# A conformer-and-attention step: the output weights of the convolution layer are split ahead of time, kept in DRAM, and used by column halves

## The chip, the cores and the metric

The kernel runs on one core of a Trainium2 chip. The metric is the device time of one execution in microseconds (us). TensorE (PE) does the matmuls, VectorE (DVE), ScalarE (ACT) and GpSimd (POOL) the elementwise work, and SyncE (SP) issues nearly all DMA transfers, in one queue of its own, in order.

## The reference, cut to what matters

Two layers over 256 context tokens (the prompt, "p") and 2048 latent tokens (the sample, "s"), width 1024. The first layer is a convolution branch, and only it and its output product matter here:

```python
def modulate(x, g, shift, scale):
    return rms_norm(x, g) * (1 + scale[:, None]) + shift[:, None]
...
    # layer 0, in words: h = modulate(x); three products of h with conv_w_in give u's two factors and z;
    # a depthwise convolution of 31 taps runs along the tokens; then
    #   y = silu(layer_norm(conv)) * silu(z);  x = x + gate * (y @ conv_w_out)
```

Everything is float32. A product of float32 matrices is made of three matmuls: each operand is split into a rounded high part and the rest, and high*high, high*low and low*high are summed.

## The kernel before

**The convolution layer** (`conv_layer`) takes the tokens in two chunks: chunk 0 holds the prompt and s0 to s1023, chunk 1 holds s1024 to s2047. Each chunk has 8 steps, one for each 128 channels (some 41 us a step in chunk 0). A step multiplies its blocks of tokens with three parts of the input weights, 24 matmuls for a block of 512 tokens (`ci_ps`, L356 to L358). DVE and ACT empty the product's PSUM banks (`u`, L456 on DVE; `z`, L459 on ACT; and others), and PE can write a bank again only when it has been emptied. The 31 taps of the step before run meanwhile: most on DVE (`cv`, L507, and the join L511), some as a scaling on ACT (`cv_p`, L485) with an addition on POOL (L488), summed and joined at the end (`cv_s`), and stored to `vc_d`. What each of PE, ACT, DVE and POOL does, and in which order, is fixed by a list of events with planned times (`at(time, piece)`); SP's queue follows from it. An engine that must wait holds back everything behind it on its list. A DVE operation that comes late so makes the ACT operation that needs it late, and with it all that stands behind that one on ACT. Weights come through two buffers of 512 KB ("raw"), and `ci_wh` (ACT, L426) and `ci_wl` (POOL) are the two halves that the matmuls read.

**The seam.** After the last step of chunk 1 the output product begins (`conv_out_pipeline`): tiles of 128 tokens, p0, p128, s0, s128 and so on, each as two column halves of 512 (a "job" below) in two quarters of 12 matmuls. A quarter takes 4 of the 8 row blocks of the weights: first `wh*yh` and `wl*yh` in turn (L826, L827), then four times `wh*yl` (L829). The layer norm of later tiles runs between the quarters; its first PE operation of a tile is the mean, `ln_s_mu` (L700), and later `ln_s_rb` (L720). The order on PE is that of the code. The output weights come through `out_weight`: eight raw loads of 512 KB, for each an ACT copy to the high part `co_h` (L752) and a DVE subtraction for the rest `co_l` (L112, helper `rest_dve`), into four buffers of 2 MB ("slot"): hi and lo of row blocks 0 to 3, and of 4 to 7. The program places this at the seam, where DVE and POOL also work on the last taps (steps 6 and 7 of chunk 1). The PSUM space of the layer norm is that of the convolution's accumulators, and comes free when the last join (`cv_7_0`, DVE L511) is done. The slots are the ones that the convolution layer used for its activations (`B[0]`, the block before the last), for the last `adaw` weights (of the modulation, used by `ada_ps`, L221), and for `ln_work`, the room in which POOL and DVE make the norm of s0.

Of the kernel before, what the change touches and what calls it, by code (L numbers as in the profile page):

```python
# [11 lines left out]
F32 = mybir.dt.float32  # L12
F32R = mybir.dt.float32r
# [5 lines left out]
P = 128  # L19
D = 1024  # L20
# [56 lines left out]
class Kern:  # L77
    def __init__(self, ctx, tc, io):
# [21 lines left out]
        self.gate_d = d("gate_d", [2, 2, D])  # L100
        self.rpb_d = d("rpb_d", [P + 1, RPB_PITCH])
        self.yp_d = d("yp_d", [NK, 2, P, NPR])


    def round_pool(self, out, src):
# [255 lines left out]
    def conv_layer(self, part_a, part_b):  # L361
# [267 lines left out]
        for j, (i, c) in enumerate([(0, 4), (0, 5)] + [(1, c) for c in range(6)]):  # L629
            g = self.ada_chunk(i, c)  # L630
            t = begin[NK + 1 + j] - ADA_TIME
            for dt in (-ADA_AHEAD, 0, 0.1, ADA_TIME - 0.5, ADA_TIME + ADA_LAG, ADA_TIME + ADA_LAG + 1.2)[: 6 if c < 4 else 5]:
                at(t + dt, step_of(g))

        for i, (load, rms, first, every, gap) in enumerate(((begin[3], begin[3] + 14, begin[3] + 26, 3.0, 30), (begin[7] + 3, begin[7] + 14, begin[8] - 7.6, 1.2, 9.6))):
            src, t0, n = part_b[i]
# [104 lines left out]
            pass  # L741
        return y[0]

    def out_weight(self, w, name, res):

        nc = self.nc
        for k in range(NK):
            if k % 4 == 0:
                hi, lo = (self.slot(F32R, f"{name}_{s}{k}", [P, NK // 2, D]) for s in "hl")
            raw = self.raw(w[k * P : k * P + P, :], [P, D], f"{name}_raw{k}")  # L750
            yield
            nc.scalar.copy(hi[:, k % 4, :], raw)  # L752
            self.rest_dve(lo[:, k % 4, :], raw, hi[:, k % 4, :])
            res[0].append(hi[:, k % 4, :])
            res[1].append(lo[:, k % 4, :])
            yield

    def conv_out(self, w, blocks, ready, res=None):

# [43 lines left out]
    def conv_out_pipeline(self, w, blocks, ready, ahead, res):  # L803
# [34 lines left out]
        def more():  # L838
            if prep:
                next(prep[0], None) or prep.pop(0)  # L840

        last = None
        for i in range(len(tiles) + 2):
            src, a = names[i]
            run = i < len(tiles)
            if run:
                x1[i] = self.t4(F32, f"x1_{src}{a}", [P, D]) if i < 2 else self.xp.tile([P, D], F32, tag="ln", name=f"x1_{src}{a}", bufs=5)
                nc.sync.dma_start(x1[i], self.tok_rows(src, a, P))
            t, before = i + 2, i + 1
            norm(t + 1, True)  # L850
            if run:
                pm = self.mm_bank(f"co_{src}{a}_0")
            if i == 0:
                quarter(i, 0, 0, pm)
                norm(t, True)
                norm(t)
            norm(t)
            norm(before)
            if 0 < i < len(tiles):
                quarter(i, 0, 0, pm)  # L860
            norm(t)
            norm(before)
            norm(t)
            norm(before)
            scale = None
            if last:
                residual(*last)
            norm(t)
            more()
            if run:  # L870
                quarter(i, 0, 1, pm)
            norm(t)
            norm(before)
            norm(t)
            if last:
                scale = self.store_x1(i - 1, names[i - 1], x1, tiles, prep, res)
                last = None
            norm(before)
            if run:
                residual(i, 0, pm)  # L880
                more()
                pm = self.mm_bank(f"co_{src}{a}_1")
                quarter(i, 1, 0, pm)
            norm(t)
            more()
            if run:
                quarter(i, 1, 1, pm)
                last = i, 1, pm
            norm(t)
            if scale:  # L890
                scale()
            norm(t + 1)
            more()
        for g in prep:
            for _ in g:
                pass
# [373 lines left out]
    def phase1(self):  # L1270
        tc = self.tc
        with ExitStack() as c:
# [5 lines left out]
            with tc.tile_pool(name="convp", bufs=2) as self.up, tc.tile_pool(name="acc", bufs=2, space=bass.MemoryType.PSUM) as self.pc:  # L1278
                E = mybir.EngineType
                ordered = {E.PE, E.Activation, E.DVE, E.Pool}  # L1280
                with tc.manual_schedule(engines=ordered):
                    self.conv_layer([("p", 0, 256), ("s", 0, 512), ("s", 512, 512)], [("s", 1024, 512), ("s", 1536, 512)])
                work = self.room[0]
                self.ready.append(self.conv_norm("s", 0, [work[:, i] for i in range(3)] + [self.t4(F32R, f"ln_s0_y{t}") for t in "hl"]))
                self.gate = [self.spread_row(self.t4(F32, f"gate0_{g}", [P, D]), self.gate_d[0, g]) for g in range(2)]
                w = [[], []]
# [77 lines left out]
    def bank(self, tag, name, bufs, n=512):  # L1364
        return self.ps.tile([P, n], F32, tag=tag, name=name, bufs=bufs)
# [394 lines left out]
```

## Time and profile before

| | |
|---|---|
| time, median of 3 runs | 2839.27 us (2832.55, 2839.27, 2840.76) |
| time of the profiled execution | 2836.73 us |
| its span from the first to the last instruction | 2834.9 us |
| PE busy | 2695.6 us, 95% of the span |
| DVE busy | 1849.0 us, 65% |
| ACT busy | 1450.4 us, 51% |
| POOL busy | 1502.8 us, 53% |
| mean granted clock of PE | 0.982 of full speed |

The shares are means over stages that differ much. The seam lies near 700 us; chunk 0 ends near 424 us. A busy PE at half clock does half the work.

### The profile page before, as it was taken

Reading aid. Unit: us, or ns where it says so; the run is one execution under the profiler, and the core shown is the slowest. Engines: PE = TensorE matmul, PEld = TensorE weight load, DVE = VectorE, ACT = ScalarE, POOL = GpSimd, SP = SyncE. Lnnn points to the kernel's source line nnn. Section 1 sums busy time; section 2 is a strip of 40 time slices with the busy share of each in tenths; the row PEclk is TensorE's granted clock in tenths of the full one; section 3 lists DMA queues with packets and bytes.
Section 4 is the critical chain, followed back from the end, with each engine's and each line's share of the span. In section 5 each row is a group of like instructions: output and inputs, shape, how many; then the busy total and the mean of one; then the engine's idle time right before and its main releaser. Section 6 shows DMA issues by size and latency. Waiting matters only on the chain. (4 is left out here: it accounts for less than half of the span.)

```text
span 2834.9 us, 45402 instructions
## 1 busy us (share of the span) xinstructions
PE 2695.6 (95%) x16079; PEld 2334.6 (82%) x16079; DVE 1849.0 (65%) x3126; ACT 1450.4 (51%) x2546; POOL 1502.8 (53%) x1631
## 2 busy tenths in 40 slices
PE   6999999999899999999999989879999999999998
PEld 4888877777677889899998878768888898888887
DVE  4789989999886510013457542157787787778885
ACT  4457565677554312134222244246676666667774
POOL 4679878888663343355113325235555555455564
PEclk9999999999899999999999999989999999999999
DMA  7233554555445554446789997788877787866753
GB/s 255 71 121 116 186 188 158 175 176 183 159 119 172 158 163 126 133 142 207 239 294 350 344 304 221 192 247 218 244 207 188 201 213 185 232 188 183 199 168 109
DMA packets 435627, 548.02 MB, mean 193 GB/s; under 512 B 42945, under 2 KB 306201, under 8 KB 435272
## 3 DMA queue, kind: packets, MB, share of 16 engines
q1 hardware_dynamic: 430080, 522.17, 61.5%
q10 hardware_dynamic: 5320, 22.95, 2.1%
q8 instruction: 128, 2.10, 0.3%
q14 instruction: 99, 0.81, 0.1%
HBM read 359.86 MB, written 189.22 MB: 194 GB/s over the span
## 5 line engine op out<-in xcount | busy, mean ns | idle before, releaser
L1514 POOL TENSOR_SCALAR sa_p<-sa_p,sa_m 128x992 f32<-128x992 f32 (+2 forms) x256 | 279.7, 1093 | 445.0 <-DVE sa_m L1513 319.0
L507 DVE SCALAR_TENSOR_TENSOR cv<-u,dw,cv 128x640 f32<-128x640 f32 (+2 forms) x570 | 427.8, 822 | 3.8 <-ACT cv L503 2.9
L1529 ACT CAST sa_pt<-sa_T 128x512 fp32r<-128x512 f32 (+3 forms) x512 | 275.2, 588 | 238.0 <-PE sa_T L1520 236.5
L112 DVE TENSOR_TENSOR sa_pt<-sa_T,sa_pt 128x512 fp32r<-128x512 f32 (+3 forms) x512 | 328.4, 682 | 3.5 <-ACT sa_pt L1529 3.0
L356 PE MATMUL ci_ps<-h_s_hi,ci_wh 128*128 128x512 f32 x768 | 307.1, 400 | 1.9 <-DVE shift L244 1.0
L358 PE MATMUL ci_ps<-h_s_hi,ci_wl 128*128 128x512 f32 x768 | 303.1, 395 | 0.0
L357 PE MATMUL ci_ps<-h_s_lo,ci_wh 128*128 128x512 f32 x768 | 302.9, 394 | 0.0
L1506 DVE TENSOR_REDUCE sa_m<-sa_S 128x1 f32<-128x512 f32 x256 | 176.1, 688 | 187.7 <-PE sa_S L1488 174.3
L1512 ACT ACTIVATE sa_p<-sa_S,sa_m 128x992 f32<-128x992 f32 (+2 forms) x256 | 267.3, 1044 | 50.7 <-DVE sa_m L1508 41.2
L1520 PE MATMUL sa_T<-ident,sa_p 128*128 128x128 f32 (+3 forms) x2048 | 272.4, 276 | 7.5 <-DVE sa_pt L112 6.8
L1520 PEld LDWEIGHTS sa_T<-ident,sa_p 128*128 128x128 f32 (+3 forms) x2048 | 239.7, 138 | 41.6 <-issue 11.3
L488 POOL TENSOR_TENSOR cv_s<-cv_s,cv_p 128x519 f32<-128x519 f32 (+1 forms) x155 | 233.2, 1504 | 69.7 <-DVE cv_s L511 48.9
L485 ACT ACTIVATE cv_p<-u,dw 128x640 f32<-128x640 f32 (+2 forms) x326 | 240.9, 770 | 54.7 <-POOL cv_s L488 35.8
L488 POOL TENSOR_TENSOR cv_p<-cv_p,cv_p 128x520 f32<-128x520 f32 (+1 forms) x155 | 227.8, 1470 | 26.7 <-ACT cv_p L485 19.1
L1549 PE MATMUL sa_O<-sa_pt,a_v 120*128 120x256 f32 (+5 forms) x1280 | 192.0, 280 | 0.0
L1544 PE MATMUL sa_O<-sa_pt,cv 128*128 128x256 f32 x1024 | 176.0, 294 | 4.2 <-DVE 1_0_of L1563 1.7
L356 PEld LDWEIGHTS ci_ps<-h_s_hi,ci_wh 128*128 128x128 f32 x768 | 145.5, 189 | 39.2 <-ACT cv_p L485 2.5
L1508 DVE CUSTOM_DVE_ANT_0 sa_S<-sa_S,a_bm,sa_m 128x480 f32<-128x480 f32 (+2 forms) x256 | 170.9, 668 | 9.1
L358 PEld LDWEIGHTS ci_ps<-h_s_hi,ci_wl 128*128 128x128 f32 x768 | 145.0, 189 | 33.6
L357 PEld LDWEIGHTS ci_ps<-h_s_lo,ci_wh 128*128 128x128 f32 x768 | 145.5, 190 | 31.1
L1549 PEld LDWEIGHTS sa_O<-sa_pt,a_v 120*128 120x128 f32 (+2 forms) x1280 | 168.8, 193 | 0.0
L356 PE MATMUL ni_s<-h_s_hi,nis_wh 128*128 128x512 f32 x384 | 152.1, 396 | 10.3 <-DVE ni_s_l L112 5.9
(843 smaller groups left out, 7181.6 us busy)
## 6 DMA issues: line engine op xcount, KB each, us to landing
adaw<-in_ada_w SPq DMA_DIRECT2D x24, 1024.0 KB
ci_w<-in_conv_w_in SPq DMA_DIRECT2D x48, 512.0 KB
a_bm<-bm_d SPq DMA_DIRECT2D x32, 720.0 KB
x_s<-in_x_sample SPq DMA_DIRECT2D x32, 512.0 KB
vs_d<-v_s SPq DMA_DIRECT2D x128, 128.0 KB
a_qh<-qh_d SPq DMA_DIRECT2D x128, 128.0 KB
a_ql<-ql_d SPq DMA_DIRECT2D x128, 128.0 KB
o_x<-x_d SPq DMA_DIRECT2D x32, 512.0 KB
```

Source lines behind the costliest of these rows:

```text
L112: self.nc.vector.tensor_tensor(out=lo, in0=src, in1=hi.bitcast(F32), op=ALU.subtract)
L356: self.nc.tensor.matmul(out, wh[:, k, :], hh[:, k, :], start=k == 0, stop=False)
L357: self.nc.tensor.matmul(out, wh[:, k, :], hl[:, k, :], start=False, stop=False)
L358: self.nc.tensor.matmul(out, wl[:, k, :], hh[:, k, :], start=False, stop=k == NK - 1)
L485: nc.scalar.activation(t, st["u"][:, c0 + tap : c1 + tap], AF.Copy, scale=self.dw[:, ct, tap : tap + 1])
L488: nc.gpsimd.tensor_tensor(out=st["sum", half], in0=st["sum", half], in1=st[half, tap], op=ALU.add)
L507: nc.vector.scalar_tensor_tensor(out=out, in0=u, scalar=w, in1=first, op0=ALU.mult, op1=ALU.add)
L1512: nc.scalar.activation(p[:, n], S[:, n], AF.Exp, scale=-1.0, bias=m[:, 2:3], accum_out=m[:, 3:4])
L1514: nc.gpsimd.tensor_scalar(out=p[:, n], in0=p[:, n], scalar1=m[:, 3:4], scalar2=1.0, op0=ALU.mult, op1=ALU.mult)
L1520: nc.tensor.transpose(t[:w, c * P : c * P + P], p[:, x + c * w : x + c * w + w], self.ident)
L1529: nc.scalar.copy(pt[:w, 0, part, :, at], t)
L1549: nc.tensor.matmul(dst, v[:w, c0 + c].rearrange("p s d -> p (s d)"), loc[:, lo:hi], start=False, stop=s == 1 and c == 3)
```

## The change

For each step k of chunk 0 a new generator, `split_out_weight(k)`, loads 128 rows of the output weights into a raw buffer, rounds them on ACT in two column halves, subtracts on DVE in place, and stores both parts to DRAM (`cw_d`, 8 MB in all, in 24 stores). `out_weight` then only loads: 16 transfers of 512 KB from `cw_d` into the four slots, a column half at a time. The first three tiles take turns: their jobs (tile, column half) run in the order (p0,0), (p128,0), (s0,0), (p0,1), (p128,1), (s0,1). The last sums of the modulation (`adat_ps`, `adao` and its store) move from the seam to the end of the pipeline's second round. The norm of s0 gets another buffer for its result.

```diff
+        for k in range(NK):
+            g = self.split_out_weight(k)
+            for dt in (15.0, 11.0, 10.0, 9.0):
+                at(begin[k + 1] - dt, step_of(g))
...
-    def out_weight(self, w, name, res):
-
-        nc = self.nc
-        for k in range(NK):
-            if k % 4 == 0:
-                hi, lo = (self.slot(F32R, f"{name}_{s}{k}", [P, NK // 2, D]) for s in "hl")
-            raw = self.raw(w[k * P : k * P + P, :], [P, D], f"{name}_raw{k}")
-            yield
-            nc.scalar.copy(hi[:, k % 4, :], raw)
-            self.rest_dve(lo[:, k % 4, :], raw, hi[:, k % 4, :])
...
+    def split_out_weight(self, k):
+
+        nc = self.nc
+        rows = slice(k * P, k * P + P)
+        raw = self.raw(self.io["conv_w_out"][0][rows, :], [P, D], f"co_raw{k}")
+        yield
+        his = []
+        for h in range(2):
+            cs = slice(h * 512, h * 512 + 512)
+            hi = self.st(F32R, f"co_h{k}_{h}", [P, 512])
+            nc.scalar.copy(hi, raw[:, cs])
+            nc.sync.dma_start(self.cw_d[0, rows, cs], hi.bitcast(F32))
+            his.append(hi)
+        yield
+        for h in range(2):
+            cs = slice(h * 512, h * 512 + 512)
+            self.rest_dve(raw[:, cs].bitcast(F32R), raw[:, cs], his[h])
+            if h == 0:
+                yield
+        nc.sync.dma_start(self.cw_d[1, rows, :], raw)
+
+    def out_weight(self):
+
+        tiles = [[self.slot(F32R, f"co_{s}{q}", [P, NK // 2, D]) for s in "hl"] for q in range(2)]
+        for h in range(2):
+            cs = slice(h * 512, h * 512 + 512)
+            for q in range(2):
+                for e in range(0, 4, 2):
+                    for s in range(2):
+                        r0 = (4 * q + e) * P
+                        src = self.cw_d[s, r0 : r0 + 2 * P, cs].rearrange("(k p) n -> p k n", p=P)
+                        self.nc.sync.dma_start(tiles[q][s][:, e : e + 2, cs].bitcast(F32), src)
+        return [[tiles[k // 4][s][:, k % 4, :] for k in range(NK)] for s in range(2)]
...
+        jobs = {0: [(0, 0), (1, 0)], 1: [(2, 0), (0, 1)], 2: [(1, 1), (2, 1)]}
...
+            if i == 1:
+                next(self.last_sums, None)
...
-                self.ready.append(self.conv_norm("s", 0, [work[:, i] for i in range(3)] + [self.t4(F32R, f"ln_s0_y{t}") for t in "hl"]))
+                y = self.slot(F32R, "ln_s0_y", [P, 2, NK, P], False)
+                self.ready.append(self.conv_norm("s", 0, [work[:, i] for i in range(3)] + [y[:, i] for i in range(2)]))
...
-                for _ in self.out_weight(self.io["conv_w_out"][0], "co", w):
-                    pass
+                w = self.out_weight()
```

**SP's queue at the seam.** The names: `vc_d` is the store of a finished convolution, `zc_d` that of `z`, `x_p` and `ln_s_v` are loads for the residual and for the norm. Before:

```order
L515 DMA vc_d<-cv_6_1_s 128x519
L461 DMA zc_d<-z_7_0_6323 128x512
L340 DMA co_raw_6523<-in_conv_w_out 128x1024
L340 DMA co_raw_6527<-in_conv_w_out 128x1024
L848 DMA x_p_6623<-in_x_prompt 128x1024
L686 DMA ln_s_v<-vc_d 128x8x128
L461 DMA zc_d<-z_7_1_6373 128x512
L232 DMA adao_5_6414<-in_ada_b 2x512
L340 DMA co_raw_6533<-in_conv_w_out 128x1024
```

And now (`co_h_6595` and `co_l_6596` are the two parts of row blocks 0 to 3, `co_h_6597` and `co_l_6598` those of 4 to 7):

```order
L516 DMA vc_d<-cv_6_1_s 128x519
L783 DMA co_h_6595<-cw_d 128x2x512
L783 DMA co_l_6596<-cw_d 128x2x512
L462 DMA zc_d<-z_7_0_6412 128x512
...
L783 DMA co_l_6596<-cw_d 128x2x512
L694 DMA ln_s_v<-vc_d 128x8x128
L462 DMA zc_d<-z_7_1_6462 128x512
L783 DMA co_h_6597<-cw_d 128x2x512 x4
L783 DMA co_l_6598<-cw_d 128x2x512 x4
L516 DMA vc_d<-cv_7_0_s 128x520
```

In the lines left out stand six more loads of row blocks 0 to 3. All eight of these (both column halves) go ahead of the first load of row blocks 4 to 7, and the four `co_l_6598` come last, ahead of the last two `vc_d`.

**POOL at the seam.** `ln_s_yh` and `ln_s_yl` are the two parts of the norm of s0, read from `ln_work`. Before, ahead of the additions of step 7:

```order
L106 TENSOR_SCALAR ln_s_yh<-ln_work 128x1024
L488 TENSOR_TENSOR cv_6_1_s<-cv_6_1_s,cv_6_1_p_6219 128x519
L109 TENSOR_TENSOR ln_s_yl<-ln_work,ln_s_yh 128x1024
L488 TENSOR_TENSOR cv_6_1_s<-cv_6_1_s,cv_6_1_p_6226 128x519
```

And now, as `ln_s_y`:

```order
L489 TENSOR_TENSOR cv_7_0_p_6396<-cv_7_0_p_6396,cv_7_0_p_6454 128x520
L107 TENSOR_SCALAR ln_s_y<-ln_work 128x1024
L489 TENSOR_TENSOR cv_7_0_p_6396<-cv_7_0_p_6396,cv_7_0_p_6459 128x520
L110 TENSOR_TENSOR ln_s_y<-ln_work,ln_s_y 128x1024
L489 TENSOR_TENSOR cv_7_0_p_6396<-cv_7_0_p_6396,cv_7_0_p_6467 128x520
```

The pair has moved behind six and seven of the eleven additions `cv_7_0_p`. The buffer `ln_work` becomes the slot of `co_l_6598`, so these four loads can only be issued behind the second of the pair.

**DVE in chunk 0**, near the end of step 4, with `cv_3_0_s` the join of the step before. Before:

```order
L112 TENSOR_TENSOR h_s_lo<-m_s_1_h_2365,h_s_hi 128x256
L507 SCALAR_TENSOR_TENSOR cv_3_0_0_2246<-u_3_1634,dw,cv_3_0_0_2246 128x640
L507 SCALAR_TENSOR_TENSOR cv_3_0_s<-u_3_1634,dw,cv_3_0_1_2251 128x640
L507 SCALAR_TENSOR_TENSOR cv_3_0_0_2246<-u_3_1634,dw,cv_3_0_0_2246 128x640
L112 TENSOR_TENSOR h_s_lo<-m_s_1_h_2405,h_s_hi 128x256
L511 SCALAR_TENSOR_TENSOR cv_3_0_s<-cv_3_0_0_2246,more,cv_3_0_s 128x640
```

And now:

```order
L113 TENSOR_TENSOR h_s_lo<-m_s_1_h_2412,h_s_hi 128x256
L113 TENSOR_TENSOR co_raw_2401<-co_raw_2401,co_h_0_2448 128x512
L508 SCALAR_TENSOR_TENSOR cv_3_0_0_2291<-u_3_1668,dw,cv_3_0_0_2291 128x640
L113 TENSOR_TENSOR co_raw_2401<-co_raw_2401,co_h_1_2451 128x512
L508 SCALAR_TENSOR_TENSOR cv_3_0_s<-u_3_1668,dw,cv_3_0_1_2296 128x640
L508 SCALAR_TENSOR_TENSOR cv_3_0_0_2291<-u_3_1668,dw,cv_3_0_0_2291 128x640
L113 TENSOR_TENSOR h_s_lo<-m_s_1_h_2458,h_s_hi 128x256
L512 SCALAR_TENSOR_TENSOR cv_3_0_s<-cv_3_0_0_2291,more,cv_3_0_s 128x640
```

Two subtractions of 128x512 now stand ahead of the join, as in each of the eight steps of chunk 0.

## Rows read from the trace of the kernel before

**Rows 1.** Page, the head: the span of the profiled execution.

```profile
span 2834.9 us, 45402 instructions
```

**Rows 2.** Windows at the seam: length, then busy PE, PEld, DVE, ACT, POOL; PEclk; DMA; GB/s.

```profile
710.00:720.00 10.00, 7.83 (x17) 4.15 (x17) 10.00 (x14) 6.75 (x10) 7.68 (x5) 0.68 0.64 210
720.00:730.00 10.00, 4.11 (x7) 2.21 (x8) 9.13 (x11) 5.69 (x9) 9.61 (x6) 0.67 0.43 136
```

**Rows 3.** Timeline of PE at the seam: start, duration, instruction [idle before, releaser].

```profile
701.90 0.39 PE L357 MATMUL ci_ps<-h_s_lo,ci_wh 128*128 128x512 f32 x1
702.14 0.40 PE L358 MATMUL ci_ps<-h_s_hi,ci_wl 128*128 128x512 f32 x1
702.46 1.93 PE L221 MATMUL ada_ps<-adaw,cs 128*32 128x512 f32 x16
710.87 1.87 PE L230 MATMUL adat_ps<-adam,sel 128*2 128x512 f32 x2 [6.49 <-ACT adam L226]
712.67 0.80 PE L826 MATMUL co_p<-co_h,ln_y 128*128 128x512 f32 x1
...
739.25 0.49 PE L700 MATMUL ln_s_mu<-ln_s_s,ones 128*128 128x128 f32 x2 [1.45 <-DVE cv_s L511]
```

**Rows 4.** Windows: the granted clock when the first output matmul begins.

```profile
710.00:712.00 2.00, 1.13 (x2) 0.09 (x2) 2.00 (x4) 2.00 (x5) 1.92 (x2) 0.50 1.09 333
```

**Rows 5.** The tile view of `co_raw`: durations (min/median/max ns), starts, who waited.

```profile
L752 ACT CAST co_h<-co_raw x8: 1028/1046/1054, 691.4 to 725.6; 128x1024 fp32r<-128x1024 f32 x8
L112 DVE TENSOR_TENSOR co_l<-co_raw,co_h x8: 1207/1434/2314, 701.4 to 727.3; 128x1024 fp32r<-128x1024 f32 x8
...
  PE co_p L827: 4.8, 4
```

**Rows 6.** Timeline of DVE at the seam.

```profile
719.24 0.75 DVE L507 SCALAR_TENSOR_TENSOR cv<-u,dw,cv_p 128x520 f32<-128x520 f32 x1
...
723.99 2.07 DVE L112 TENSOR_TENSOR co_l<-co_raw,co_h 128x1024 fp32r<-128x1024 f32 x1 [0.87 <-ACT co_h L752]
...
738.44 0.75 DVE L511 SCALAR_TENSOR_TENSOR cv_s<-cv,more,cv_s 128x520 f32<-128x520 f32 x1
```

**Rows 7.** Timeline of POOL: additions alone, the parts of s0, additions at the seam.

```profile
661.13 8.24 POOL L488 TENSOR_TENSOR cv_p<-cv_p,cv_p 128x520 f32<-128x520 f32 x6 [1.05 <-ACT cv_p L485]
...
686.67 1.06 POOL L106 TENSOR_SCALAR ln_s_yh<-ln_work 128x1024 fp32r<-128x1024 f32 x1
...
688.96 2.40 POOL L109 TENSOR_TENSOR ln_s_yl<-ln_work,ln_s_yh 128x1024 fp32r<-128x1024 f32 x1
...
698.15 18.63 POOL L488 TENSOR_TENSOR cv_p<-cv_p,cv_p 128x520 f32<-128x520 f32 x11
```

**Rows 8.** Timeline of SP: the last raw load of the output weights.

```profile
721.14 0.33 SPq L340 DMA_DIRECT2D co_raw<-in_conv_w_out  x1
```

**Rows 9.** Windows in which long loads queue up: columns as in rows 2.

```profile
10.00:15.00 5.00, 0.00 (x0) 0.00 (x0) 1.74 (x4) 4.34 (x8) 2.64 (x7) 1.00 1.03 403
741.00:746.00 5.00, 5.00 (x24) 4.14 (x23) 1.83 (x3) 2.10 (x3) 0.37 (x1) 1.00 0.89 288
```

**Rows 10.** Windows in chunk 0, steps 3 to 6: columns as in rows 2.

```profile
210.00:330.00 120.00, 119.36 (x635) 101.62 (x634) 119.63 (x149) 77.07 (x120) 102.18 (x73) 1.00 0.40 136
```

**Rows 11.** Timelines of ACT, PE and DVE in chunk 0.

```profile
271.43 0.80 ACT L503 ACTIVATE cv<-u,dw 128x640 f32<-128x640 f32 x1 [2.04 <-DVE cv_s L511]
...
275.23 0.56 ACT L459 COPY z<-ci_ps 128x512 f32<-128x512 f32 x1
...
275.85 0.50 PE L356 MATMUL ci_ps<-h_s_hi,ci_wh 128*128 128x512 f32 x1 [0.64 <-ACT z L459]
...
331.69 0.42 DVE L456 TENSOR_TENSOR u<-ci_ps,u 128x256 f32<-128x256 f32 x1 [1.24 <-PE ci_ps L358]
```

**Rows 12.** Timelines of SP and ACT in chunk 0: a load of input weights, and its copy.

```profile
272.31 0.40 SPq L340 DMA_DIRECT2D ci_w<-in_conv_w_in  x1
...
278.31 1.05 ACT L426 CAST ci_wh<-ci_w 128x1024 fp32r<-128x1024 f32 x1
```

More of the change, by code (lines that the diff above doesn't have):

```diff
@@ L102, in __init__ @@
         self.yp_d = d("yp_d", [NK, 2, P, NPR])
+        self.cw_d = d("cw_d", [2, D, D])
     def round_pool(self, out, src):
@@ L840, in more @@
                 next(prep[0], None) or prep.pop(0)
+        jobs = {0: [(0, 0), (1, 0)], 1: [(2, 0), (0, 1)], 2: [(1, 1), (2, 1)]}
         last = None
         for i in range(len(tiles) + 2):
-            src, a = names[i]
             run = i < len(tiles)
-            if run:
-                x1[i] = self.t4(F32, f"x1_{src}{a}", [P, D]) if i < 2 else self.xp.tile([P, D], F32, tag="ln", name=f"x1_{src}{a}", bufs=5)
-                nc.sync.dma_start(x1[i], self.tok_rows(src, a, P))
+            job = jobs.get(i, [(i, 0), (i, 1)]) if run else []
+            for k in sorted({k for k, _ in job} - set(x1) if i < 3 else {k for k, _ in job}):
+                src, a = names[k]
+                x1[k] = self.t4(F32, f"x1_{src}{a}", [P, D]) if k < 2 else self.xp.tile([P, D], F32, tag="ln", name=f"x1_{src}{a}", bufs=5)
+                nc.sync.dma_start(x1[k], self.tok_rows(src, a, P))
+            bank = lambda k, h: self.mm_bank(f"co_{names[k][0]}{names[k][1]}_{h}")
             t, before = i + 2, i + 1
@@ L851, in conv_out_pipeline @@
             if run:
-                pm = self.mm_bank(f"co_{src}{a}_0")
+                pm = bank(*job[0])
             if i == 0:
-                quarter(i, 0, 0, pm)
+                quarter(*job[0], 0, pm)
                 norm(t, True)
@@ L859, in conv_out_pipeline @@
             if 0 < i < len(tiles):
-                quarter(i, 0, 0, pm)
+                quarter(*job[0], 0, pm)
             norm(t)
@@ L864, in conv_out_pipeline @@
             norm(before)
-            scale = None
+            scales = []
             if last:
@@ L870, in conv_out_pipeline @@
             if run:
-                quarter(i, 0, 1, pm)
+                quarter(*job[0], 1, pm)
             norm(t)
@@ L874, in conv_out_pipeline @@
             norm(t)
-            if last:
-                scale = self.store_x1(i - 1, names[i - 1], x1, tiles, prep, res)
-                last = None
+            if last and last[1]:
+                scales.append(self.store_x1(last[0], names[last[0]], x1, tiles, prep, res))
+            last = None
             norm(before)
             if run:
-                residual(i, 0, pm)
+                residual(*job[0], pm)
+                if job[0][1]:
+                    scales.append(self.store_x1(job[0][0], names[job[0][0]], x1, tiles, prep, res))
                 more()
-                pm = self.mm_bank(f"co_{src}{a}_1")
-                quarter(i, 1, 0, pm)
+                pm = bank(*job[1])
+                quarter(*job[1], 0, pm)
             norm(t)
@@ L886, in conv_out_pipeline @@
             if run:
-                quarter(i, 1, 1, pm)
-                last = i, 1, pm
+                quarter(*job[1], 1, pm)
+                last = *job[1], pm
             norm(t)
-            if scale:
+            for scale in scales:
                 scale()
```

8 lines of the change are left out of this document (3 added, 5 removed).

## The prediction

> **What bounds the kernel now.** The page's head gives a span of 2834.9 us [rows 1]; the execution took 2836.73 us. PE is busy 95% of it, so I looked for the stretch in which PE loses most, with the windows and then the timelines. It is the seam between the convolution layer and the output product. The last layer matmul starts at 702.14, the modulation's 16 matmuls take 1.93 us, PE idles 6.49 us, and the output product begins at 712.67 [rows 3]. In the windows 710 to 730 PE is busy 7.83 and 4.11 us of 10, at a granted clock of 0.68 and 0.67 [rows 2]; at the first output matmul the clock is 0.50, the 1.2 GHz level, after the idle time [rows 4].
>
> A measure of the loss: `ln_s_mu` starts at 739.25 [rows 3], 37.1 us after the last layer matmul. Ahead of it stand 48 output matmuls (p0, both halves). A matmul of this size follows the next in 0.24 us (701.90 to 702.14 [rows 3]; 0.23 over longer rows), so 48 of them are 11 us; the modulation is 1.9 and `adat_ps` some 1 us. About 23 us are lost. The tile view says what PE waits for inside: `co_l` from DVE, 4.8 us in four waits there alone [rows 5]. DVE in turn is busy 10.00 and 9.13 us of 10 [rows 2], and the end of the stretch is DVE's too: `ln_s_mu` waits 1.45 us for the last join [rows 3], which runs at 738.44 [rows 6].
>
> **The change, part by part: the seam.** Away go eight ACT copies (8 x 1.046 = 8.4 us), eight DVE subtractions (8 x 1.434 = 11.5 us by the median, which lies between 1.207 and 2.314) [rows 5] with an idle 0.87 us [rows 6], and eight raw loads. In come 16 loads of 0.524 MB. What is the new bound? Three candidates for the start of `ln_s_mu`, which again has two jobs (48 matmuls) ahead of it: the loads, DVE, POOL.
>
> *Loads.* The first slot pair is `B[0]`, used by the last block but one. The last block's 24 matmuls take 24 x 0.23 = 5.5 us, so the pair is free at 702.14 - 5.5 = 696.6. The other two slots come later: one behind the modulation's matmuls (702.46 + 1.93 = 704.4 [rows 3]), the last behind POOL's second part of s0's norm. POOL's eleven additions began at 698.15; with the pair (1.06 + 2.40) gone from ahead of them they begin near 694.7. Six additions last 6 x 1.37 = 8.2 (six undisturbed took 8.24), then come the pair and one addition: 694.7 + 8.2 + 3.5 + 1.4 = 707.8, or 709 with some additions at the 1.69 us that they take at the seam (18.63 / 11) [rows 7]. As eight loads of row blocks 0 to 3 go first, the queue does not run dry: 4.19 MB take over 10 us.
>
> Then bytes decide. Ahead of the first needed `co_l` piece of row blocks 4 to 7 stand 8 + 4 loads, a load of `ln_s_v` (0.52 MB) and two `zc_d` stores (0.52), with itself 7.9 MB. For a deep queue the windows show 403 GB/s at best, and 288 where stores and loads alternate [rows 9]. To this comes a fixed part: the last raw load was issued at 721.14 [rows 8] and its copy ran at 725.6 [rows 5], 4.5 us in all, of which 0.52 MB is 1.3 at 403: at most 3.2; I take 2.4. At 403 the piece lands at 696.6 + 2.4 + 19.6 = 718.6; at 288 at 696.6 + 2.4 + 27.4 = 726.4. I take 380, nearer the fast row, since these are loads in a deep queue with few stores among them: 696.6 + 2.4 + 20.8 = 719.8.
>
> PE does (p0,0)'s first quarter at 704.4 to 707.2, then waits until 719.8. It starts again at half clock, as it did here after its idle stretches [rows 4]: 12 matmuls x 0.46 = 5.5, then 24 at 0.23 = 5.5 (with 1 us more where the clock is still low). `ln_s_mu` comes at 719.8 + 5.5 + 6.5 = 731.8, at 730.6 by the fast end and 738.4 by the slow one.
>
> *DVE and POOL.* POOL's sum of eleven is complete at 694.7 + 3.5 + 15.1 = 713.3 (18.6 instead of 15.1 at the seam's pace: 716.8). DVE's last chain began at 719.24 and ended at 739.2, with three subtractions and the idle 0.87 inside [rows 6]; without them (3 x 1.434 + 0.87 = 5.2) it lasts 14.8 us: it ends at 728.1 to 731.6. So the loads are the later ones, by up to 4 us, and DVE's freed time is worth only what they leave.
>
> The gain at `ln_s_mu` is 739.25 - 731.8 = 7.4, between 0.9 and 8.7. Behind it the steady alternation of jobs and norms goes on as before, so I let the gain stand, less 0.7 us for the next job's PSUM bank, which now waits for DVE's residual, because `adat_ps` takes a bank further on. **Seam: 6.7 us gained**, 0 to 8.
>
> **The change, part by part: chunk 0.** Sixteen subtractions of 128x512, half of the ones in rows 5: 0.60 us at best, 0.72 by the median, 1.16 at worst. Sixteen ACT copies of half of 1.046 us: 8.4 us in 330; ACT is busy 77.07 us of 120 in steps 3 to 6 [rows 10], and where they stand in step 4 it idles. I put them at nothing; without that cover they cost up to 1 us a step. The 24 stores and eight raw loads (12 MB) meet a DMA share of 0.40 [rows 10].
>
> DVE isn't free. From 210 to 330 it is busy 119.63 us of 120 [rows 10]. So subtractions placed there are not hidden; they make all later DVE work late, until an idle gap, the next being 1.24 us at 331.69 [rows 11]. Who waits for it? At the end of step 4, DVE's join lets an ACT operation start at 271.43 after 2.04 us of idle ACT; behind it on ACT stands the copy of `z` at 275.23, and PE has already idled 0.64 us for that copy at 275.85 [rows 11]. There is no slack: DVE's lateness goes on to PE one to one. The order rows put two subtractions ahead of this join, and the pair of step 3, near 219, lies in the same saturated stretch. Four subtractions: 4 x 0.72 = 2.9 us, 2.4 at best, 4.6 at worst. After that stall all engines have shifted alike; the pair of step 5 (1.4) is about what the gap at 331.69 takes up, and pairs of other steps lie ahead of idle gaps of DVE of several us. **Chunk 0: 2.9 us lost**, 1 to 5, the 1 in case earlier waits already take in a part.
>
> Trainium skill, "SBUF — State Buffer", section "Who interferes with whom": a VectorE instruction with two SBUF inputs contends with a GpSimd instruction that reads SBUF. The subtractions are of that kind and POOL's additions read SBUF; POOL is busy 102.18 us of 120 there [rows 10], and the spread of the seam's subtractions, 1.207 to 2.314 us [rows 5], agrees. By the rule alone each of the four would stand at the long end: 4 x 1.16 = 4.6 instead of 2.9, and the whole change would give 2834.6 by the profiled execution.
>
> **Sum.** -6.7 + 2.9 = -3.8 us against 2836.73: 2832.9. The profiled execution lies 2.5 us under the median of the runs (2839.27), which would give 2835.5. I forecast 2834, between the two.
>
> **Rivals.** 0.3% of 2839, 8.5 us, is about what a measurement of this kernel can tell from no change.
> - *The forecast*: the loads end the wait, chunk 0 gives back nearly half. Within 8.5 us. With its bounds (-8 + 1 to 0 + 5, on either base) 2830 to 2844. 0.60.
> - *The loads come early and the rest follows.* For: 403 GB/s is on record [rows 9], and DVE loses 12 us of work at the seam. Then DVE's join bounds `ln_s_mu` at 728.1: 11.1 us gained, and with POOL's additions no longer beside subtractions the following tiles may run 2 us more ahead. Less 1 in chunk 0: -10 to -12, 2825 to 2829. It decides if the piece lands by 716.5, which needs over 440 GB/s by the sum above, or a queue that serves the needed pieces out of turn. Against: no window shows it. 0.22.
> - *The loads come late.* At 288 GB/s [rows 9] the wait ends at 726.4 and the gain is 0.9 - 0.7; with chunk 0's 2.9 it ends 3 us slower, 2842: within. It is the forecast's slow end and holds 0.1 of its 0.60.
> - *Chunk 0 turns from hidden to bound* (slower). The split holds one of the two raw buffers for some 10 us of each step, from its load to its last store, and the next loads of input weights then queue on SP behind these. Such a load was issued at 272.31 for a copy at 278.31 [rows 12], and in other steps 20 us ahead; by the new order it goes out behind the store of the rest, about 3 us later, and lands with 3 us left or less. If POOL's and DVE's mutual slowing eats these 3 us, PE waits in each of seven steps: 2 us each are 14, plus 2.9, less 6.7: +10, 2847 to 2850. It decides from a lateness of 3 us on. 0.18.
>
> **How the numbers follow.** Likeliest: 2834. Its own range is 2830 to 2844. With half of the fast rival and the near end of the slow one the range of 8 in 10 is 2826 to 2847. Faster by over 0.3%: 0.22 and a part of the forecast's fast end, 0.27. Slower: 0.17. Same: 0.56.
>
> **What would show each step.** In the changed profile: PE idle some 12 us for a DMA of `co_l` between the first two quarters, near 707 to 720, and half clock after it; `ln_s_mu` near 732 plus chunk 0's delay (counted from the last layer matmul: 29.7 us instead of 37.1); DVE idle before its last chain; near 275 a PE wait of 3.5 instead of 0.64 us for ACT's `z`, and the last layer matmul some 3 us later than 702.14. Wrong would be: waits of PE for `ci_wh` in several steps, `ln_s_mu` released by DVE, or a lead at `ln_s_mu` that is gone some tiles later.

## The result and the profile after

The changed kernel takes 2847.07 us (median of 18 runs, 2837.9 to 2854.99), the kernel before, beside it, 2837.77 (18 runs, 2825.78 to 2844.85). The ratio is 1.0034, with an interval of 1.0024 to 1.0044: slower by some 0.3%, where no change or a small gain was forecast. The profiled execution took 2849.59 us. The page's head [rows 1]:

```profile
span 2847.8 us, 45500 instructions
```

PE is busy 2694.8 us in it, 0.8 less than before, so as a sum the time has gone into waits. To find where, I set each PE matmul of the changed kernel against the same one before. The first 100 us differ by -4.3 us, which I don't put down to the change: in the profiles of the other kernels below they lie between -4.3 and +1.7, in no order (e4 apart). From there the lateness jumps twice, by 5.6 us at 275 (-4.3 to +1.3) and by 6.7 at 640 (+1.1 to +7.8). At the seam it falls by 7.4 and rises again by some 6. Behind 1300 us it drifts by several us, differently in each profile.

PE's timeline at these places (start, duration, instruction, [idle before, releaser]; [rows 3, 11]):

```profile
275.10 0.80 PE L357 MATMUL ci_ps<-h_s_hi,ci_wh 128*128 128x512 f32 x1 [4.17 <-ACT z L460]
...
639.26 0.49 PE L708 MATMUL ln_s_mu<-ln_s_s,ones 128*128 128x128 f32 x2 [1.00 <-DVE ln_s_s L700]
642.64 0.80 PE L357 MATMUL ci_ps<-h_s_hi,ci_wh 128*128 128x512 f32 x1 [2.89 <-ACT u L455]
...
709.68 0.40 PE L359 MATMUL ci_ps<-h_s_hi,ci_wl 128*128 128x512 f32 x1
...
723.93 0.79 PE L854 MATMUL co_p<-co_h,ln_y 128*128 128x512 f32 x1 [7.21 <-DMA co_h<-cw_d]
729.36 0.79 PE L855 MATMUL co_p<-co_l,ln_y 128*128 128x512 f32 x1 [4.63 <-DMA co_l<-cw_d]
...
739.49 0.38 PE L708 MATMUL ln_s_mu<-ln_s_s,ones 128*128 128x128 f32 x2
...
766.08 0.33 PE L301 MATMUL m_p_t<-ident,x_p 128*128 128x128 f32 x1 [1.94 <-POOL x_p L943]
767.66 0.36 PE L301 MATMUL m_p_t<-ident,x_p 128*128 128x128 f32 x1 [1.26 <-POOL x_p L943]
```

The windows there, columns as in [rows 2]:

```profile
276.00:278.00 2.00, 2.00 (x6) 1.52 (x6) 2.00 (x3) 2.00 (x4) 1.92 (x2) 0.50 0.72 216
642.00:644.00 2.00, 1.36 (x3) 1.17 (x4) 1.97 (x4) 2.00 (x3) 1.92 (x2) 0.50 1.05 362
...
704.00:710.00 6.00, 6.00 (x27) 4.54 (x25) 6.00 (x9) 3.07 (x5) 5.69 (x5) 1.00 0.94 269
710.00:720.00 10.00, 5.46 (x29) 2.51 (x28) 6.78 (x11) 6.43 (x10) 9.77 (x8) 1.00 1.06 384
720.00:730.00 10.00, 1.44 (x3) 0.84 (x4) 9.85 (x14) 5.23 (x8) 9.45 (x9) 0.50 1.06 383
```

**Place one, 275 us.** The wait for ACT's `z` has grown from 0.64 [rows 11] to 4.17 us. That is 3.5 of the 5.6; the other 2.1 lie in the next microseconds, where PE is busy at a granted clock of 0.50, the 1.2 GHz level. ACT waits for the join, the join stands behind two subtractions, and beside the first runs a POOL instruction. The timelines of ACT, of DVE and of POOL:

```profile
270.69 0.80 ACT L504 ACTIVATE cv<-u,dw 128x640 f32<-128x640 f32 x1 [5.57 <-DVE cv_s L512]
```

```profile
263.06 2.90 DVE L113 TENSOR_TENSOR co_raw<-co_raw,co_h 128x512 fp32r<-128x512 f32 x1
...
266.67 1.27 DVE L113 TENSOR_TENSOR co_raw<-co_raw,co_h 128x512 fp32r<-128x512 f32 x1
```

```profile
262.81 2.60 POOL L110 TENSOR_TENSOR ci_wl<-ci_w,ci_wh 128x1024 fp32r<-128x1024 f32 x1
```

ACT's idle time was 2.04 before [rows 11]. The two subtractions last 2.90 + 1.27 = 4.17 us where 1.44 was forecast (that PE's wait has the same length is chance). All sixteen, in the tile view (min/median/max ns):

```profile
L113 DVE TENSOR_TENSOR co_raw<-co_raw,co_h x16: 681/1270/2895, 89.2 to 393.0; 128x512 fp32r<-128x512 f32 x16
```

**Place two, 640 us**, is far from both the split and the seam. Here PE has another order: the mean of s0's norm stands ahead of the second block of 24 matmuls of the step, where before it stood behind the fourth, at 654.23. DVE's reduction for it so runs ahead of `gs`. PE's mean before; then DVE after (with the last join of the seam, for below), and before:

```profile
654.23 0.38 PE L700 MATMUL ln_s_mu<-ln_s_s,ones 128*128 128x128 f32 x2
```

```profile
637.25 1.95 DVE L700 TENSOR_REDUCE ln_s_s<-ln_work 128x128 f32<-128x1024 f32 x1 [1.51 <-DMA ln_work<-vc_d]
...
642.91 0.16 DVE L245 TENSOR_TENSOR gs<-adat_ps,more 128x8 f32<-128x8 f32 x1
...
734.79 0.75 DVE L512 SCALAR_TENSOR_TENSOR cv_s<-cv,more,cv_s 128x520 f32<-128x520 f32 x1
```

```profile
637.24 0.17 DVE L244 TENSOR_TENSOR gs<-adat_ps,more 128x8 f32<-128x8 f32 x1 [0.94 <-PE adat_ps L237]
...
642.02 2.05 DVE L692 TENSOR_REDUCE ln_s_s<-ln_work 128x128 f32<-128x1024 f32 x1 [4.32 <-DMA ln_work<-vc_d]
```

The mean waits 1.00 us for the reduction. The block behind it then takes the bank that ACT empties with `u`, which comes late, behind a table load, and PE waits 2.89 us more. The table load stood ahead of this `u` before the change too (638.47, for 1.28 us), and no wait of PE came of it there:

```profile
640.69 1.28 ACT L455 ACT_TABLE_LOAD   x1
641.99 0.60 ACT L455 ACTIVATE u<-ci_ps 128x512 f32<-128x512 f32 x1
```

Both waits and the half clock behind them make up the 6.7 us.

**The seam.** From the last layer matmul (709.68) to the mean (739.49) it takes 29.8 us, where it took 37.1: the forecast was 29.7. PE waits for loads, in two pieces, 7.21 and 4.63 us, and no longer for the last join (734.79 in DVE's rows above). SP's rows show a gap between the issues of the two groups of loads, a store of `z` whose issue takes 4.37 us. The DMA engines were not idle in it (share 1.06 in both windows from 710 to 730), so no run shows that this gap made the loads land later:

```profile
704.28 0.37 SPq L783 DMA_DIRECT2D co_h<-cw_d  x1
...
712.20 4.37 SPq L462 DMA_DIRECT2D zc_d<-z  x1
716.97 2.81 SPq L783 DMA_DIRECT2D co_h<-cw_d  x4
719.89 3.33 SPq L783 DMA_DIRECT2D co_l<-cw_d  x4
```

But of the lead of 7.4 us, 1.1 goes at the moved sums, 3.7 at 766, where PE waits for POOL's `x_p` before it transposes, and 0.8 in the slow matmuls right behind; the 157th to the 409th output matmul have a lead of 1.7 to 1.8 left. (All leads here: the time from the last layer matmul to the output matmul of that number in the kernel before, less the same time in the kernel in question.) Even that isn't clearly the seam's: e5 below, with the old seam behind a late layer, has 1.6 by this measure from the mean on.

What the transposes wait for begins beside a POOL instruction too. DVE's last addition to p128's `x_p` (the like one at 752.08 takes 0.69 us) and the POOL instruction next to it:

```profile
759.37 2.90 DVE L864 TENSOR_TENSOR x_p<-x_p,co_op 128x512 f32<-128x512 f32 x1
```

```profile
759.23 2.48 POOL L110 TENSOR_TENSOR ln_s_yl<-ln_s_v,ln_s_yh 128x1024 fp32r<-128x1024 f32 x1
```

ACT's square of this `x_p` follows at 762.35, POOL's scaling of `x_p` at 764.90. POOL's own next operation, which ACT waits for as well, also stands behind the 2.48 us, so how much of the wait DVE's late addition makes by itself isn't shown.

### The profile page after: what moved, and what is told of

The parts are those of the page before. It is cut to its first block, busy times and chain, and to the rows that moved or that the text cites. A ratio compares the mean times of both kernels' runs of the same rounds, so it can differ in the third digit from the quotient of the medians.

```text
span 2847.8 us, 45500 instructions
## 1 busy us (share of the span) xinstructions
PE 2694.8 (95%) x16079; PEld 2333.1 (82%) x16079; DVE 1858.0 (65%) x3134; ACT 1450.1 (51%) x2554; POOL 1498.4 (53%) x1631
## 5 line engine op out<-in xcount | busy, mean ns | idle before, releaser
L489 POOL TENSOR_TENSOR cv_s<-cv_s,cv_p 128x519 f32<-128x519 f32 (+1 forms) x155 | 230.4, 1487 | 68.0 <-DVE cv_s L512 43.9
L489 POOL TENSOR_TENSOR cv_p<-cv_p,cv_p 128x520 f32<-128x520 f32 (+1 forms) x155 | 225.8, 1457 | 31.8 <-ACT cv_p L486 24.1
```

Source lines behind the costliest of these rows:

```text
L489: nc.gpsimd.tensor_tensor(out=st["sum", half], in0=st["sum", half], in1=st[half, tap], op=ALU.add)
```

## The experiments

Each is run against the kernel before on the same chip; ratios are to it. The edits of e1 to e3, e6 to e8 and e10 give each pair of the split a time of its own, in place of the one loop; diffs are against the changed kernel unless said otherwise.

**e1: the pairs of steps 3 and 4 leave their places, the mean stays early.**

```diff
-            for dt in (15.0, 11.0, 10.0, 9.0):
-                at(begin[k + 1] - dt, step_of(g))
+            t = begin[[1, 2, 3, 3, 1, 6, 7, 8][k]] + [-10.0, -10.0, -10.0, 8.0, 8.0, -10.0, -10.0, -10.0][k]
+            for dt in (-5.0, -1.0, 0.0, 1.0):
+                at(t + dt, step_of(g))
```

> The changed kernel with two pairs of subtractions moved: those of steps 3 and 4, which lay in the stretch where VectorE has no idle time, now run in steps 1 and 3, ahead of gaps of VectorE. The early mean of s0's norm (near 640 us) stays. Theory: VectorE's lateness alone makes the 4.17 us wait near 275 us and the half clock behind it, 5.6 us in all; so that wait is 0.7 us or less, the one near 640 stays at about 3.9 us with its clock loss, and the time falls by 5 to 6 us against the changed kernel, to about 2841. Rival (the copies on ScalarE or the transfers cause the wait): the wait near 275 stays at 3 us or more. Rival (the lead is given back further on): the wait goes and the time stays within 2 us of 2847.

2843.0 us, ratio 1.0028 [1.0014, 1.0042]. The waits of PE from 250 to 360 us (total, times, longest):

```profile
PE ci_ps L357 <- ACT z L460: 1.9, 2, 1.0
```

The wait of 4.17 has become two of 1.0 and 0.9, at 278 and 354 us. At 640 us the waits of 2.9 and 1.0 are still there. The time lies lower than the changed kernel's, but the intervals overlap.

**e2: one pair (of step 5) is moved, and the mean falls back behind the fourth block.**

```diff
...
+            t = begin[[1, 2, 3, 4, 5, 7, 7, 8][k]] + [-10.0, -10.0, -10.0, -10.0, -10.0, 8.0, -10.0, -10.0][k]
...
```

> The changed kernel with only the pair of step 5 moved to step 6. By this the list that follows from the planned times puts the first operation of s0's norm on TensorE behind the fourth block again, as in the kernel before, instead of ahead of the second. Theory: the early mean is what costs 6.7 us near 640 (1.0 us for the mean's input, 2.9 us for a bank that ScalarE empties late, and half clock); so these waits go, the one near 275 stays at about 4 us, and the time falls by 6 to 7 us against the changed kernel, to about 2840.5. Rival (the order is innocent, the wait comes from transfers or from ScalarE's load): a wait of 2 us or more for ScalarE stays near 640.

2842.65 us, ratio 1.0021 [1.0008, 1.0035]. Near 640 only the 0.4 us wait for `gs` is left, and 4.1 us stay at 275. The moved pair makes a wait of its own, though; PE from 380 to 400 us:

```profile
PE ci_ps L357 <- ACT z L460: 2.9, 1, 2.9
```

So the mean's place is the cause at 640 us. As a time the run doesn't show it: its interval overlaps the changed kernel's, and the new wait hides a part.

**e3: both mended.**

```diff
...
+            t = begin[[1, 2, 3, 3, 2, 6, 7, 8][k]] + [-10.0, -10.0, -10.0, 8.0, 8.0, -10.0, -10.0, -10.0][k]
...
```

> Both moves: the pairs of steps 3 and 4 run in steps 2 and 3, and the mean stands late. Theory: the two losses add up; 12 us less than the changed kernel, 2835, that is 2 to 3 us less than the kernel before, because the seam keeps a gain of 0.7 us or more. Rival (the seam or what follows it has become slower by itself): 2840 or more, with the last layer matmul as early as before the change.

2834.21 us, ratio 0.9992 [0.998, 1.0003], clear of the changed kernel's interval. From 250 to 300 us PE waits for nothing, and the matmuls at 640 are 0.2 us early, the first 100 us aside. These two places explain the loss, and the seam's gain is still missing. From 660 to 860 us the wait at the transposes is there, as in the changed kernel:

```profile
PE m_p_t L301 <- POOL x_p L944: 3.2, 2, 1.9
```

**e4: the seam alone.** The split is replaced by copies of the raw weights from DRAM to DRAM, so both parts are the whole weights.

```diff
-            g = self.split_out_weight(k)
...
+            at(begin[k + 1] - 10.0, lambda k=k: self.keep_out_weight(k))
...
+        for s in range(2):
+            self.nc.sync.dma_start(self.cw_d[s, rows, :], self.io["conv_w_out"][0][rows, :])
```

> The seam of the changed kernel without the split: no raw load, copy or subtraction in chunk 0; the unsplit weights are copied from DRAM to DRAM in its place, so both parts that the product uses are the whole weights and the output is another. Theory: chunk 0 and the layer run as before the change, and the seam alone is worth what the profile of the changed kernel shows, 7 us at the mean of the norm, of which 1 to 3 us are left after some tiles: 2835 to 2837. If the loads alone bound the seam, the first piece of the later row blocks' low part arrives 19 to 20 us after the last layer matmul. Rival (the copies' 8 MB in chunk 0 cost by themselves): over 2840.

2863.69 us, ratio 1.0093 [1.008, 1.0107]. As a time it tells nothing of the seam: SP issued the copies, which wait for nothing, from 21.93 to 44.65 us, ahead of the last two of the eight `adaw` loads of the start. PE from 0 to 100 us, where the changed kernel waits 12.3 us for `adaw`:

```profile
PE ada_ps L222 <- DMA adaw<-in_ada_w: 31.0, 4, 17.9
```

Within the trace it serves. With no split in chunk 0, the lead at the mean is again 7.4 us, and it falls to 1.9 by the 157th output matmul and 1.3 by the 277th. So the loss behind the seam doesn't come from the split.

**e5: the split alone.** The kernel before, with the split in chunk 0, whose result is stored and not used.

```diff
...
+        for k in range(NK):
+            g = self.split_out_weight(k)
+            for dt in (15.0, 11.0, 10.0, 9.0):
+                at(begin[k + 1] - dt, step_of(g))
...
```

> The kernel before, with the split in chunk 0 added and its result left unused; the output weights are still split a second time at the seam. Theory: all losses of the change lie in what the split does to the layer: the wait near 275 us (4.2 us and half clock, 5.6 in all), about 1 us near 400 and the early mean near 640 (6.7), so at the last layer matmul it stands 11 to 13 us behind the kernel before (apart from the first 100 us, which differ from run to run), the seam takes its old 37 us, and the time is 2847 to 2850. Rival (the changed seam carries a part of the loss): 2842 or less.

2848.4 us, ratio 1.0042 [1.0026, 1.0058]: some 12 us. Both places are there. PE from 250 to 300, and from 600 to 660 us:

```profile
PE ci_ps L357 <- ACT z L460: 4.1, 1, 4.1
```

```profile
PE ci_ps L357 <- ACT u L455: 3.0, 1, 3.0
PE ln_s_mu L706 <- DVE ln_s_s L698: 0.8, 1, 0.8
```

So the split by itself moves the mean, over 240 us behind its last subtraction. From the last layer matmul to the mean this kernel takes 35.5 us, not 37.1: that is the 1.6 named above, with a seam that nobody changed.

**e6: e3, and the last transposes of round 2 are left to later blocks** (`more()` is the step that issues the next piece of the attention layer's work).

```diff
...
-            more()
+            if i != 2:
+                more()
```

> The kernel of e3 with one call left out: the first pair of transposes of the next layer's input stands one round later in TensorE's order. Theory: the lead of the seam, 6.9 us at the norm's mean, is lost to the waits of these transposes for GpSimd's scaling of p128 (1.94 and 1.26 us, and the clock's dip); so these waits go, and of the lead some 5 us are left in the steady pipeline instead of 1.2: 2830.5. Rival (the pipeline behind it is bound by the norm's chain on VectorE and ScalarE): another wait takes its place within 60 us and the lead is 1 to 2 us as before.

2828.36 us, ratio 0.9974 [0.9961, 0.9986]. PE from 660 to 860 us:

```profile
PE co_p L855 <- DMA co_h<-cw_d: 7.3, 1, 7.3
PE co_p L856 <- DMA co_l<-cw_d: 5.5, 2, 4.6
PE ln_s_var L720 <- DVE ln_s_s L701: 2.0, 3, 0.9
```

The transposes' wait is gone, and the lead stays: 6.2 us at the 205th output matmul, 8.2 at the 397th (e3: 1.2 at both). This kernel is faster than the kernel before and than the changed one.

**e7: e3, with the loads in the order of the code**, the first column half of all row blocks ahead of the second.

```diff
...
-                w = self.out_weight()
+                with tc.manual_schedule(engines={E.SP}):
+                    w = self.out_weight()
```

> The kernel of e3 with the 16 loads issued in the order in which the code names them: both parts of all row blocks for column half 0 first, then column half 1. Theory: the order of the loads, not their bytes as such, sets the wait between the first two quarters: some 2 MB that are not yet needed no longer go ahead. The first low piece of the later row blocks arrives 14 to 16 us after the last layer matmul instead of 19.6, and the norm's mean starts 26 to 27 us after it instead of 30.2, then bound by VectorE's last join. At the transposes the lead is lost again down to about 1 us: 2833 to 2834. Rival (the rate falls, or the slots come free too late): the pieces arrive within 1 us of where they did.

2835.88 us, ratio 1.0006 [0.9992, 1.0021]. PE from 660 to 860 us:

```profile
PE ln_s_mu L709 <- DVE cv_s L512: 6.5, 1, 6.5
PE co_p L856 <- DMA co_l<-cw_d: 3.8, 3, 2.4
...
PE co_p L855 <- DMA co_h<-cw_d: 1.7, 1, 1.7
```

DVE's timeline at the end of its last chain:

```profile
719.00 0.68 DVE L864 TENSOR_TENSOR co_op<-co_p,gate 128x512 f32<-128x512 f32 x1
...
720.93 1.27 DVE L865 TENSOR_TENSOR x_p<-x_p,co_op 128x512 f32<-128x512 f32 x1
...
730.09 0.76 DVE L512 SCALAR_TENSOR_TENSOR cv_s<-cv,more,cv_s 128x520 f32<-128x520 f32 x1
```

PE waits 5.5 us for loads instead of 13.4, and 6.5 for the last join. The jobs that end sooner hand DVE their residuals (two pairs, 4.0 us in all) ahead of that join, which here begins 28.8 us behind the last layer matmul (701.30); in the changed kernel it does so after 25.1. About 1.4 of the 3.7 us between them lie ahead of DVE's last chain, which begins when POOL's sum is done (11.9 us behind the last layer matmul, against 10.4). So the mean's lead is 7.2 us, where e3 has 6.9, and behind the transposes nothing is left of it: 1.7 us late.

**e8: e6 and e7 together, with the last step's stores of `z` issued by ACT.**

```diff
...
-                        nc.sync.dma_start(self.zc_d[ct * P : ct * P + P, c : c + n], z)
+                        (nc.scalar if chunk and ct == NK - 1 else nc.sync).dma_start(self.zc_d[ct * P : ct * P + P, c : c + n], z)
```

> e6 and e7 together, and the last step's two stores of z issued by ScalarE, since SyncE waits 4.4 us for the second of them ahead of the loads of the later row blocks. Theory: the lead at the norm's mean grows to 11 us or more and is kept behind the transposes: 2824 to 2827, 0.3 to 0.5% less than the kernel before. Rival (VectorE's and GpSimd's last taps bound the seam): the mean waits for VectorE's join, 28 us after the last layer matmul, and the time is no lower than that of e6.

2834.73 us, ratio 0.9997 [0.9985, 1.001]. The mean waits 6.0 us for DVE, the lead is 7.8 at the mean and 4.2 to 7.1 later, and yet the time isn't below e6's. In the two profiles the difference lies in the drift behind 1300 us, which I can't put down to an instruction; it stays open.

**e9: the subtraction becomes a copy, with one input.** The kernel leaves out the subtraction, so the second part is the high part again.

```diff
...
-            self.rest_dve(raw[:, cs].bitcast(F32R), raw[:, cs], his[h])
+            self.nc.vector.tensor_copy(raw[:, cs].bitcast(F32R), his[h])
```

> The split's subtraction, which reads two tiles, becomes a VectorE copy that reads one (the remainder kept in DRAM is then the high part again, so the output is another); all other instructions stay, but the mean of the s0 norm falls back into its late place in the layer, as in e2. Theory: the subtraction is long because it reads two inputs while GpSimd reads two of its own; the copies then last at most 0.75 us each, the longest under 1 us, ScalarE's wait ahead of the 275 us place falls from 5.6 to at most 3.5 us, TensorE's wait there from 4.2 to at most 2.5, and the whole comes to about 2838 us (no wait near 640 us). Rival: it is the number of VectorE operations in the step, whatever they read; then the copies last as long as the subtractions, or the wait stays at 3.5 us or more, and the time is about 2842.

2838.47 us, ratio 1.0008 [0.9995, 1.0022]. The copies (tile view) are as uneven as the subtractions, and PE's wait at 275 is 3.2 us, between the two expectations:

```profile
L768 DVE CAST co_raw<-co_h x16: 416/999/2632, 94.8 to 396.8; 128x512 fp32r<-128x512 f32 x16
```

So it isn't the second input. The timelines told what it is; DVE and POOL of this run:

```profile
268.16 2.63 DVE L768 CAST co_raw<-co_h 128x512 fp32r<-128x512 f32 x1
```

```profile
267.91 2.60 POOL L110 TENSOR_TENSOR ci_wl<-ci_w,ci_wh 128x1024 fp32r<-128x1024 f32 x1
```

POOL's instruction ends at 270.51, the copy at 270.79, 0.28 later. Of the 14 copies that begin within a POOL instruction, 13 end 0.28 to 0.29 us behind it; the other one began 0.01 us ahead of its end. In the changed kernel the same holds for the subtractions: 14 of the 16 begin so, and 13 of them end 0.55 us behind the end of POOL's instruction (263.06 + 2.90 is 0.55 behind 262.81 + 2.60); the other one began 0.05 us ahead of that end. They don't run slower; they stand until POOL is done. POOL stands in turn: its eight additions (L489) that begin during a subtraction last 1.90 to 2.11 us, where 1.57 is usual.

**e10: e6's two edits with other places for the pairs**, two in each of four steps.

```diff
...
+            t = begin[(1, 1, 2, 2, 3, 3, 7, 7)[k]] + (-10.0, 8.0)[k % 2]
...
+            if i != 2:
+                more()
```

> The split's pairs are moved to the layer's steps 1, 1, 2, 2, 3, 3, 7, 7, one early and one late in each, and the last transposes of the weight load are left to later blocks as in e6. Theory (the loss in chunk 0, the mean's place and the transposes are three losses that can be taken away one by one): as e6, 2826 to 2830 us, a ratio of 0.996 to 0.998. Rival: e6's gain came from where its eight pairs happen to stand; then this one is at 2832 or more.

2829.04 us, ratio 0.9984 [0.9974, 0.9994]: faster again, though less clearly. In chunk 0 it keeps waits for `z` of 1.1 and 1.4 us; the lead behind the seam is 5.5 to 8.4.

**e11: the subtraction becomes a reduction over an axis of length one.** As in e9, the second part is the high part again; the copies on ACT and the transfers stay.

```diff
...
+            self.nc.vector.tensor_reduce(out=raw[:, cs], in_=his[h].bitcast(F32).rearrange("p (n x) -> p n x", x=1), axis=AX.X, op=ALU.add)
```

> The split's subtraction becomes a VectorE reduction over an axis of length one: one input, the same 128x512 in and out, the same place in the order (the remainder kept in DRAM is then the high part again, so the output is another); the mean of the s0 norm stays in its early place, as in the changed kernel. Theory: a subtraction, or the copy of the run before, does not run until the GpSimd instruction that is under way has ended, and a reduction does not wait so. Then all 16 reductions last alike (longest less than 0.3 us over the shortest, some 0.6 to 1.1 us each), ScalarE's idle time near 270 us falls from 5.6 to at most 4, TensorE's wait there from 4.2 to at most 2.5, and the time comes to 2840 to 2844. Rival: any VectorE instruction on two SBUF tiles is lengthened there; then the reductions beside GpSimd's work also last up to 2.6 us or more, TensorE's wait stays over 3 us, and the time is that of the changed kernel, 2847.

2841.59 us, ratio 1.0023 [1.0011, 1.0034]. The tile view, and the timelines of DVE, POOL and PE at the same place as above:

```profile
L768 DVE TENSOR_REDUCE co_raw<-co_h x16: 675/680/686, 94.1 to 392.0; 128x512 f32<-128x512 f32 x16
```

```profile
267.06 0.68 DVE L768 TENSOR_REDUCE co_raw<-co_h 128x512 f32<-128x512 f32 x1
```

```profile
266.82 2.60 POOL L110 TENSOR_TENSOR ci_wl<-ci_w,ci_wh 128x1024 fp32r<-128x1024 f32 x1
```

```profile
276.48 0.50 PE L357 MATMUL ci_ps<-h_s_hi,ci_wh 128*128 128x512 f32 x1 [0.67 <-ACT z L460]
```

All sixteen last alike, the one beside the 2.60 us POOL instruction too. As many DVE operations, as long as a free subtraction (0.68), in the same places: and PE waits 0.67 us, as before the change [rows 11], with ACT idle 2.07. The place at 275 costs nothing; the waits at 640 (2.7) and at the transposes remain, and with them the time, 2841.59. The loss in chunk 0 is DVE standing behind POOL, not DVE's added work, ACT's copies or the transfers.

## Why the prediction was wrong

**The seam's mean: right.** 29.8 us against 29.7, and PE's waits for the loads 11.8 us against "some 12" (7.2 of them for `co_h`, where I had named `co_l` alone). That the sum fits so well is luck, since two errors cancel: the piece of `co_l` came 19.7 us behind the last layer matmul (17.7 forecast); and the 36 matmuls from there to the mean took 10.1 us, not the 12.0 that I had priced with the half clock. The rate that I took, 380, is that of the windows from 710 on, 383 and 384 GB/s; but from 704 to 710, where the first loads share the engines with stores, it was 269. Over six us that difference is worth 1.8, an estimate of where the 2.0 went; no run isolates it. That DVE would be done up to 4 us ahead of the loads holds too: its join ends at 735.54, the mean starts at 739.49. But these 4 us can't be had by earlier loads alone, as e7 shows.

**The step that failed first: "I let the gain stand".** I priced the lead behind the mean at -0.7 and followed it no further. It runs into the moved sums and into transposes that wait for POOL; 7.4 us become 1.8. e4 shows the loss without the split, e6 takes it away. With all three losses gone (e6) the change is worth 7.5 us (2835.85 to 2828.36), about the seam's lead: the gain was there to be had. e10 bears that out with less; e8 doesn't, as a time, though at 1300 us both are some 9 us ahead of the kernel before. That the lead might be gone some tiles later I had named as what would prove me wrong, and had given no price.

**The second: "Four subtractions: 4 x 0.72 = 2.9 us".** It measured 5.6, over my worst case of 4.6 (5 for the range). The price came from halving [rows 5], whose spread I read as contention that makes an operation longer in proportion (the four longest of those eight all end 1.08 us behind a POOL instruction). It is a wait for another engine's instruction: its size is what is left of that instruction, up to 2.35 us, and has nothing to do with the size of the subtraction. Of the other part, "lateness goes on to PE one to one", e11 shows the opposite for plain DVE work: four operations of 0.68 us ahead of the join cost PE nothing. And DVE's 119.63 us of 120 [rows 10], from which I took that DVE isn't free, contain such waits, which look busy. The profile before shows them: of the sixteen `h_s_lo` in these 120 us (128x256, 0.42 us alone) fourteen begin within a POOL instruction and end 0.28 to 0.30 us behind it, and together the sixteen last 16.3 us instead of 6.6. One of them on DVE, and POOL beside it:

```profile
224.35 1.67 DVE L112 TENSOR_TENSOR h_s_lo<-m_s_h,h_s_hi 128x256 fp32r<-128x256 f32 x1
```

```profile
223.32 2.41 POOL L109 TENSOR_TENSOR ci_wl<-ci_w,ci_wh 128x1024 fp32r<-128x1024 f32 x1
```

So 9.7 of the 119.63 us were waits for POOL. That e11's reductions found their room there is likely, but not shown. Last, I left out the half clock behind the wait, 2.1 us.

I had drawn on the section that says so: the Trainium skill, "SBUF — State Buffer", section "Who interferes with whom". There the shared port pair is an exclusive lock for a whole instruction, and the loser fully blocks; a DVE instruction with two SBUF inputs and a copy can take part, a `tensor_reduce` on trn2 never. The runs agree in all three (0.55 us behind POOL's end; 0.28 behind it; 0.68 flat). I priced the subtractions with the longest one seen before, where the longest POOL instruction beside it was the thing to look up.

**The third, and the largest: a step without a price.** The mean of s0's norm moves in the order, for 6.7 us, in a stretch that the change doesn't touch. The place isn't one of the events with planned times. I read order rows where the diff had edits, and not where it had none. That the split moves it is shown (e5), and that moving one pair puts it back (e2); why the placing of one depends on the other stays open.

**The sum.** 5.6 + 6.7 - 1.8 = 10.5 us against 9.3 measured (2847.07 - 2837.77); forecast were 2.9 - 6.7. The drift behind 1300 us stands outside this sum. My rival on the slower side had +10 by another mechanism, PE waiting for `ci_wh` in several steps; no such wait appears, so its nearness to the time is luck.

## What to carry to other kernels

Before a DVE operation is placed, look at what POOL runs at that place: its price may be the rest of POOL's instruction, and "busy" on DVE may be such a wait. A gain at one point of a pipeline is worth what is left of it two stages on: follow the lead to the next operation that another engine releases, and ask what it waits for. And compare the order of the whole program, the stretches without an edit too.

## What the runs showed of the hardware

- A 128x512 f32 subtraction on DVE takes 0.68 us alone; begun while POOL works on SBUF, it ends 0.55 us behind POOL's instruction, 13 of 14. At the seam before, of six subtractions of 128x1024 that begin so, four end 1.08 us behind it; beside the other two it is POOL that stands (2.39 and 3.39 us, where 1.37 is usual). A one-input copy of the same shape (0.42 alone) does so too, 0.28 behind, 13 of 14 (e9). A reduction (0.68) doesn't wait (e11), and neither do the 537 taps `cv<-u,dw,cv` between 80 and 700 us (at most 0.89 us), whose accumulator is in PSUM; the fifteen `cv<-u,dw,cv_p`, which read `cv_p` from SBUF in its place, last up to 2.19.
- A wait of PE of 4.17 us cost 2.1 us more, at a granted clock of 0.50 in the window behind it.
- With the DMA engines busy throughout (share 1.06), the issue of one store on SP took 4.37 us; the loads behind it were issued after that.
- In e4, 8 MB of copies from DRAM to DRAM were issued at 21.93 us, ahead of two `adaw` loads, and PE waited 31.0 us for `adaw` instead of 12.3.
